# An encoder layer in one kernel: half of the first attention's probability blocks turned by VectorE and DRAM instead of TensorE, and twelve lower weight halves computed by GpSimd during the down-projection

## The chip, the cores and the metric

The kernel runs on one core of a Trainium2 chip. The metric is device time in microseconds (us), the median of the runs shown. The engines are called by the profile's names: PE is TensorE, DVE VectorE, ACT ScalarE, POOL GpSimd, SP SyncE (here it only issues DMAs).

## The reference

One layer of a bidirectional encoder, for two sequences of 512 tokens with 1024 features, in float32:

```python
x = x + 0.5 * swiglu(rms_norm(x, ffn1_norm), ffn1_w_gate, ffn1_w_up, ffn1_w_down)   # 1024 -> 2816 -> 1024
h = rms_norm(x, mix_norm)
proj = h @ w_in      # q, k, v of the attention; q, k, v, gates of the mLSTM; output gate; two merge gates
...
a = softmax(q k^T * scale) v      # 8 heads of 64, 2 key heads; RMS norm and rotary of q and k before
m = mlstm_bidirectional(...)      # 4 heads of 128
x = x + (sigmoid(g_att) * (a @ w_up_att) + sigmoid(g_mlstm) * (m @ w_up_mlstm)) @ w_out
x = x + 0.5 * swiglu(rms_norm(x, ffn2_norm), ffn2_w_gate, ffn2_w_up, ffn2_w_down)
```

followed by a last RMS norm.

## The kernel before, in words

**Arithmetic.** A float32 operand is split into an upper half `hi` (rounded to fp32r) and a lower half `lo = x - hi`; a product is three matmuls: hi by hi, hi by lo, lo by hi. ACT makes `hi` by a copy, DVE makes `lo` by a subtraction. For weights this is `fetch_w` (the load, L271) and `split_w` (L278 on ACT, L279 on DVE); for other tiles `split` (L715 on ACT, L716 on DVE).

**Stages.** Up-projection of the first feed-forward, its down-projection (437 to 648 us), the mixing block of sequence 0 (`mix(0)`), that of sequence 1 (`mix(1)`), output projection, second feed-forward. Weights of the mixing block are used by both sequences: `load_w` (L284) loads and splits a block for sequence 0 and stores both halves to DRAM (`wpark`, L303); sequence 1 loads them back (L293).

**Down-projection.** `ffn_down` (L548) runs 28 steps, four chunks of the inner dimension by seven products of a Strassen-like scheme. A step is a set of matmuls (L632), whose right operands `rt` come from DRAM four steps ahead (L566) and whose weights are split two steps ahead (`prep`). Sums are kept in SBUF tiles (`xs`, `e16`, `e5`). At step 7 it calls `mix_consts`, which loads and scales tables on POOL (L744 to L759). In its last seven steps `done1` receives finished rows of features; for both sequences POOL adds up their squares (L155), from which DVE (L225, L226) and PE (L232) make the row statistics that `mix` begins with.

**Attention.** In `mix(s)` the attention is written out by hand, and its PE instructions are pinned to the order of the program. Per head there are four query blocks of 128: `score` (L1096) does two matmuls (L1101), the row maximum on DVE (L1104), the exponential on ACT (L1106), the reciprocal on DVE (L1107), and the scaling of the probabilities by it, on ACT for odd query blocks (L1109), else on DVE (L1111). The product with V needs the probabilities turned, keys in the partitions, one key block at a time:

- `turn_keys` (L1114): four PE transposes (L1117) into PSUM, then the hi/lo split into SBUF. Sequence 0 does this for all four key blocks of each head.
- In sequence 1, only key blocks 2 and 3 go that way. For blocks 0 and 1, `turn_early` (L1129) turns 32 x 32 squares inside the partitions on DVE into part of the tile `box`; `send` (L1133) writes them to DRAM (`abuf`) with four DMAs of 128 KB from SP's queue, in an order of rows that completes the transposition; `fetch` (L1138) reads a key block back with a DMA of 256 KB from POOL's queue, and `parts` splits it from SBUF. A head's blocks 0 and 1 are used one head later in the loop.

`values` (L1148) multiplies with V: two matmuls per key block, one step behind the turn. Between these, `among(n)` issues n matmuls of the other projections (L825, "fill"); 8 per step, 24 per weight block. A step is one score, the fill, one turn and the product of the turn before; there are four per head. In sequence 0 the fill ends with head 6, block 1; the work of the mLSTM (L804, L1292) is placed between the rest by the scheduler.

The kernel is written with a tile framework: a scheduler places instructions by priority (`shifted` moves it), keeps the pinned ones in program order, and each engine then runs its own list in order. A DMA is issued by the engine whose queue holds it, so an instruction that waits in SP's list holds up all transfers behind it.

Of the kernel before, what the change touches and what calls it, by code (L numbers as in the profile page):

```python
# [16 lines left out]
P = 128  # L17
S = 512
# [8 lines left out]
def encoder(ctx, tc, I, outs):  # L27
# [91 lines left out]
    def f(ap):  # L119
        return ap.bitcast(F32)  # L120
# [160 lines left out]

    WEIGHTS = 60

    parked = {}  # L284

    def load_w(view, key, park=True):


        if key in parked:
            d, shape = parked[key]  # L290
            w2 = wpool.tile(shape, F32R, tag="w8", bufs=4, name=nm("w"))
            for i in range(2):
                nc.sync.dma_start(f(w2[:, i]), d[:, i])  # L293
            return w2[:, 0], w2[:, 1]
        raw = fetch_w(view)
        with shifted(-WEIGHTS):
            hi, lo = split_w(raw, V_)
        if not park:
            return hi, lo
        shape = [P, 2] + list(raw.shape[1:])  # L300
        parked[key] = d, _ = dpool.tile(shape, F32, name=nm("wpark")), shape
        for i, t in enumerate((hi, lo)):
            nc.sync.dma_start(d[:, i], f(t))  # L303
        return hi, lo
# [240 lines left out]
    DH = KD // 2  # L545
    n_steps = len(DOWN) * len(CHUNKS)

    def ffn_down(wd, rb, ring, tail, xres, done, at_step, hook, turned=None):  # L548
        n = n_steps
        rt = [A([P, 4, 2, S], F32R, "rt") for _ in range(3)]  # L550
        e16 = xs[2] = A([P, KD, S], F32, "e16")
        xs[0], xs[1] = A([P, KD, S], F32, "xs"), A([P, KD, S], F32, "xs")
        e5 = A([P, DH, S], F32, "e5")
        right = [[t[:, q] for q in range(3)] for t in rt] + [[t[:, 3] for t in rt]]
        w8 = [wpool.tile([P, 2, 2, S], F32R, tag="w8", bufs=4, name=nm("w")) for _ in range(4)]
        units = [t[:, i] for t in w8 for i in range(2)]
# [2 lines left out]
        free = [(0, t[:, 0:S], t[:, S:D]) for t in wr] + [(1, va, ha), (1, *v2)]  # L559
        s1s = ring.rows["s"]  # L560
        at = [0, 0]

        def load_right(i):
            if i < n:
# [131 lines left out]
        for i in range(n):  # L696
            if i == n - 1 and turned:
                products_turned(i)
            else:
                products(i, whole)  # L700
            prep(i + 2)
            load_right(i + 4)
            if i == 1:
                free.extend((1, *h4[k:k + 2]) for k in (0, 2))
                refill()
            if i == at_step:
                hook()

    def normed(xt, g, R, d):

# [137 lines left out]
    def mix(s, xh, xl, early=None, extra=None, after=None):  # L848
# [248 lines left out]
        def score(h, b):  # L1097
            hk = h // 4
            p = PS()
            for j in range(2):  # L1100
                pin(nc.tensor.matmul(p, qT[:, h, b * P:(b + 1) * P], kv[:, hk * 2 + j, :],  # L1101
                                     start=(j == 0), stop=(j == 1)))
            c = small(3, "asm")
            V_.tensor_reduce(c[:, 0:1], p, axis=AX.X, op=ALU.max, negate=True)  # L1104
            e = T2()
            nc.scalar.activation(e, p, AF.Exp, bias=c[:, 0:1], accum_out=c[:, 1:2])  # L1106
            V_.reciprocal(c[:, 2:3], c[:, 1:2])  # L1107
            if b % 2 and (s or h or b < 3):
                nc.scalar.activation(e, e, AF.Copy, scale=c[:, 2:3])  # L1109
            else:  # L1110
                V_.tensor_scalar(e, e, c[:, 2:3], None, op0=ALU.mult)  # L1111
            return e

        def turn_keys(Ps, kb):  # L1114
            p = PT()
            for b in range(4):
                pin(nc.tensor.transpose(p[:, b * P:(b + 1) * P], Ps[b][:, kb * P:(kb + 1) * P], ident))  # L1117
            return parts(p.rearrange("p (i a m) -> p a i m", i=4, a=4) if s else p)

        def parts(p):  # L1120
            ph, pl = T2(F32R), T2(F32R)
# [17 lines left out]
            return parts(p)  # L1139

        pos = {}
        KBS = (2, 3, 0, 1) if s else (0, 1, 2, 3)

        def values(h, kb, pp):
            if kb == KBS[0]:
                pos[h] = PO()
            for i, w in enumerate(pp):
                pin(nc.tensor.matmul(pos[h], Vst[:, kb, h // 4, :], w, start=(kb == KBS[0] and i == 0),  # L1148
                                     stop=(kb == KBS[3] and i == 1)))
            if kb != KBS[3]:  # L1150
                return
            po = pos.pop(h)
            order = ((lambda t: t.rearrange("p (a i m) -> p i a m", i=4, a=4)),
                     (lambda t: t.rearrange("p (i a m) -> p i a m", i=4, a=4))) if s else (lambda t: t,) * 2
            if h % 2 == 0:
                afs[0] = T2(F32, "f2")
            af = afs[0]
            o0 = (h % 2) * DA
            o1 = DA - o0
            t = T2(F32, "f2")  # L1160
            was, now = order
            nc.scalar.activation(now(t[o0:o0 + DA, :]), was(po[o1:o1 + DA, :]), AF.Copy)
            V_.tensor_tensor(now(af[o0:o0 + DA, :]), was(po[o0:o0 + DA, :]), now(t[o0:o0 + DA, :]), op=ALU.add)
            if h % 2:
                split(af, att[:, h // 2, 0, :], att[:, h // 2, 1, :])
# [20 lines left out]
        for b in range(4):  # L1186
            Ps.append(score(0, b))
            next(rope, None)
            among(FIRST[b])
        if s:  # L1190
            for i in range(2):
                turn_early(Ps[i], i)
        last = None
        for h in range(HA):
            nxt = []
            for b in range(4):
                if h in (0, 2, 4) and b == 2:
                    q_turn(h // 2 + 1, pin)
                if (h, b) == (0, 1):
                    gate_tops(*tops)  # L1200
                if (h, b) in ((0, 3), (2, 3)):
                    rope = q_rope(h // 2 + 2)
                if h < 4:
                    next(rope, None)
                if h + 1 < HA:
                    nxt.append(score(h + 1, b))
                if s and (h, b) != (HA - 1, 3) and b in (3, 0):
                    if b == 3:
                        for i in range(2):
                            turn_early(nxt[i], i)  # L1210
                    else:
                        for i in range(2, 4):
                            turn_early(Ps[i], i)
                if s and b == 1:
                    send(h)
                n0, n1_ = FILLER if b else SOON
                among(n0)
                pp = None
                if not s or b > 1:
                    pp = h, b, turn_keys(Ps, b)  # L1220
                elif h:
# [7 lines left out]
            Ps = nxt  # L1229
        for b in range(2 * s):  # L1230
            pp = HA - 1, b, fetch(HA - 1, b)
            among(sum(FILLER))
            values(*last)
            last = pp
# [515 lines left out]
        normed(xt, gm, R[1], d)  # L1750
        split(xt, nhl[1][0][:, d, :], nhl[1][1][:, d, :])

    ffn_down(I["ffn1_w_down"][0], rbuf[0], up.ring, tail, xbuf, done1, 7, mix_consts)


    box()
# [199 lines left out]
```

## Time and profile before

| | |
|---|---|
| median of 3 runs | 2035.45 us (2035.37 to 2037.29) |
| profiled execution: its own time | 2037.6 us |
| profiled execution: span of the trace | 2035.8 us |
| PE instructions | 9185 |
| first down-projection, from the first to the last product | 437.5 to 648 us |
| first attention, from the first turn to the last | 717.6 to 811.0 us |
| second attention, from the first turn on DVE | 1080.8 us on |

Times inside the program are counted from the start of the span. A row of a timeline gives start, duration, engine, line, operation, `written<-read` tiles, shapes and count. Matmuls are pipelined: the duration of one overlaps the next, so that their cost is the distance of their starts. In a row on idle time the engine waited for what stands behind the arrow. A row of the windows view gives, for a stretch of time, the busy time of each engine with its number of instructions, then the granted PE clock, the mean busy share of the DMA engines and GB/s. Rows of one line (`xN: min/median/max`) give durations in ns.

### The profile page before, as it was taken

How to read it: one execution, taken by the hardware profiler on the slowest of the kernel's cores; microseconds unless marked ns; L12 is line 12 of the kernel's file. 1: busy time of each engine (PE TensorE's matmuls, PEld its weight loads, DVE VectorE, ACT ScalarE, POOL GpSimd, SP SyncE). 2: the span in 40 equal slices, each digit the busy share in tenths (PEclk: the TensorE clock that was granted, in tenths of full speed). 3: DMA queues.
4: the chain of work that ended last, by engine and by line, in shares of the span. 5: the costliest groups of instructions: out<-in, count | busy, mean ns of one | idle time of the engine just before them, and what ended most of it. 6: DMA issues, size and time to landing. Idle time of an engine off the chain costs nothing.

```text
span 2035.8 us, 26777 instructions
## 1 busy us (share of the span) xinstructions
PE 2020.2 (99%) x9185; PEld 1665.7 (82%) x9185; DVE 1584.0 (78%) x2828; ACT 921.5 (45%) x1675; POOL 111.1 (5%) x148
## 2 busy tenths in 40 slices
PE   9999999999999999999999999999999999999998
PEld 7888888888888888888888877888888888888887
DVE  7988888886797798776566867467798988786797
ACT  7644444442234577653325654245444444442224
POOL 0000000001003000100120000011000000000001
PEclk9999999999999999999999999999999999999999
DMA  9656565799766954868656668877565655689753
GB/s 312 197 171 216 177 218 182 237 334 364 271 214 225 294 169 148 259 208 302 211 166 209 214 189 268 274 228 228 173 206 166 217 177 179 205 332 352 269 196 119
DMA packets 334696, 462.17 MB, mean 227 GB/s; under 512 B 21384, under 2 KB 207840, under 8 KB 333280
## 3 DMA queue, kind: packets, MB, share of 16 engines
q1 hardware_dynamic: 329920, 446.08, 65.8%
q0 software_dynamic: 4480, 14.11, 2.0%
q8 instruction: 72, 1.18, 0.2%
q14 instruction: 64, 0.52, 0.1%
q10 hardware_dynamic: 160, 0.27, 0.0%
HBM read 292.44 MB, written 167.94 MB: 226 GB/s over the span
## 4 chain that ended last, share of the span: by engine, by line
PE 91%; DVE 3%; DMA 3%; ACT 2%; issue 1%; SPq 0%; DVEq 0%; ACTq 0%
PE mm L839 13%; PE pso L374 12%; PE pst L374 12%; PE mm L374 10%; PE mm L632 9%; PE pss L374 6%; PE pst L632 4%; PE pss L632 4%; PE mm L825 4%; PE mm L804 3%; PE pso L632 3%; PE pso L1148 1%; PE pss L1101 1%; PE pst L839 1%; PE pss L839 1%; PE pso L1360 1%
## 5 line engine op out<-in xcount | busy, mean ns | idle before, releaser
L374 PE MATMUL pst<-xc,w 128*128 128x512 f32 x1056 | 253.8, 389 | 1.2 <-ACT t L409 1.2
L374 PEld LDWEIGHTS pst<-xc,w 128*128 128x128 f32 x1056 | 198.1, 188 | 42.7 <-ACT t L409 1.6
L374 PE MATMUL mm<-xc,w 128*128 128x512 f32 x972 | 229.6, 390 | 1.6 <-ACT f L382 1.6
L374 PEld LDWEIGHTS mm<-xc,w 128*128 128x128 f32 x972 | 182.0, 188 | 39.6 <-ACT f L382 2.1
L632 PE MATMUL mm<-rt,w 128*128 128x512 f32 x765 | 178.7, 389 | 0.0
L839 PE MATMUL mm<-xh,w 128*128 128x512 f32 x560 | 176.1, 391 | 1.4 <-DMA w<-wpark 1.4
L332 ACT ACTIVATE w<-t 128x512 fp32r<-128x512 f32 x176 | 106.5, 627 | 135.7 <-issue 63.1
L632 PEld LDWEIGHTS mm<-rt,w 128*128 128x128 f32 x765 | 143.5, 188 | 29.8
L333 DVE TENSOR_TENSOR w<-t,w 128x512 fp32r<-128x512 f32 x176 | 117.8, 688 | 40.9 <-ACT w L332 39.1
L374 PE MATMUL pso<-xc,f 128*128 128x512 f32 x528 | 127.0, 389 | 0.0
L374 PE MATMUL pss<-xc,w 128*128 128x512 f32 x528 | 126.8, 389 | 0.0
L374 PE MATMUL pso<-xc,w 128*128 128x512 f32 x528 | 126.8, 389 | 0.0
L839 PEld LDWEIGHTS mm<-xh,w 128*128 128x128 f32 x560 | 104.8, 188 | 23.7 <-DMA w<-wpark 1.8
L374 PEld LDWEIGHTS pso<-xc,f 128*128 128x128 f32 x528 | 99.0, 188 | 21.0 <-DVE t L413 0.4
L374 PEld LDWEIGHTS pso<-xc,w 128*128 128x128 f32 x528 | 99.1, 188 | 20.6
L374 PEld LDWEIGHTS pss<-xc,w 128*128 128x128 f32 x528 | 99.1, 188 | 20.6
L825 PE MATMUL mm<-xh,w 128*128 128x512 f32 x336 | 111.9, 398 | 0.0
L839 PE MATMUL mm<-xl,w 128*128 128x512 f32 x280 | 109.6, 391 | 0.0
L715 ACT ACTIVATE w<-wr 128x512 fp32r<-128x512 f32 x72 | 45.1, 632 | 138.4 <-PE pso L632 64.8
L278 ACT ACTIVATE w<-wr 128x1024 fp32r<-128x1024 f32 (+1 forms) x64 | 65.3, 1030 | 80.4 <-issue 24.5
L279 DVE TENSOR_TENSOR w<-wr,w 128x1024 fp32r<-128x1024 f32 (+1 forms) x64 | 79.8, 1247 | 26.6 <-ACT w L278 15.7
L715 ACT ACTIVATE w<-t 128x512 fp32r<-128x512 f32 x82 | 51.8, 632 | 107.4 <-PE pst L632 62.4
(457 smaller groups left out, 4080.4 us busy)
## 6 DMA issues: line engine op xcount, KB each, us to landing
rt<-rbuf SPq DMA_DIRECT2D x154, 512.0 KB, 5.4
wpark<-w SPq DMA_DIRECT2D x88, 512.0 KB, 3.6
w<-wpark SPq DMA_DIRECT2D x88, 512.0 KB, 5.3
wr<-in_ffn_w_gate_dram SPq DMA_DIRECT2D x62, 512.0 KB, 5.4
rbuf<-tab SPq DMA_DIRECT2D x102, 256.0 KB, 4.0
wr<-in_ffn_w_up_dram SPq DMA_DIRECT2D x44, 512.0 KB, 4.6
rbuf<-f SPq DMA_DIRECT2D x72, 256.0 KB, 4.2
wr<-in_w_in_dram SPq DMA_DIRECT2D x36, 512.0 KB, 5.7
```

Source lines behind the costliest of these rows:

```text
L278: pin(nc.scalar.activation(hi, raw, AF.Copy))
L279: pin(lo_eng.tensor_tensor(lo, raw, f(hi), op=ALU.subtract))
L332: pin(nc.scalar.activation(t[:, 0], src, AF.Copy))
L333: pin(V_.tensor_tensor(t[:, 1], src, f(t[:, 0]), op=ALU.subtract))
L374: nc.tensor.matmul(p, a[:, k, :], xt[:, b, k, :], start=(first and k == 0 and i == 0), stop=(k == HK_ - 1 and i == 2), skip_group_check=True)
L632: nc.tensor.matmul(p, u[:, a, d * P:(d + 1) * P], r[:, b, ts], start=(first and q == 0 and k == 0), stop=(q == len(us) - 1 and k == 2), sk ...
L715: nc.scalar.activation(hi, src, AF.Copy)
L804: mark(nc.tensor.matmul(p[b][:, :N], a[:, k, bs], w_[:, kl, :], start=(k == 0 and i == 0), stop=(k == KD - 1 and i == 2)), (kl, b, i) == ( ...
L825: pin(nc.tensor.matmul(p[0], a[:, k, :], b, start=(k == 0 and i == 0), stop=(k == n - 1 and i == 2)))
L839: mark(nc.tensor.matmul(p, a[:, k, :], b, start=(k == 0 and i == 0), stop=last), last)
L1101: pin(nc.tensor.matmul(p, qT[:, h, b * P:(b + 1) * P], kv[:, hk * 2 + j, :], start=(j == 0), stop=(j == 1)))
L1148: pin(nc.tensor.matmul(pos[h], Vst[:, kb, h // 4, :], w, start=(kb == KBS[0] and i == 0), stop=(kb == KBS[3] and i == 1)))
```

## The change

Three parts, all for sequence 0 (line numbers after the change are higher by 8 to 26):

1. **Turns.** In the first attention, heads 0 to 6 turn key blocks 0 and 1 as sequence 1 does: 28 turns on DVE, 28 sends, 14 fetches. Head 7 keeps PE transposes for all four blocks, blocks 0 and 1 behind the loop. The order of blocks in a head becomes 2, 3, 0, 1, and the copies out of PSUM permute the columns as in sequence 1.
2. **Scaling.** In sequence 0, heads 1 to 7 scale all four query blocks on ACT: 14 scalings move from DVE to ACT.
3. **Lower halves.** For twelve blocks of `w_in` (columns 896 and 1408, six gates of the attention, four output gates of the mLSTM) the lower half is computed in the down-projection of the first feed-forward, one block per step from step 3 on, by POOL: a load of 512 KB, a cast to fp32r (128x1024), a subtraction, a store of 512 KB to `wpark`. The space is the second half of the tile of `e5`, which is made twice as large. In `mix(0)`, `load_w` loads the block and splits off the upper half on ACT as before, but loads the lower half from `wpark` on SP instead of computing it on DVE, and stores only the upper half.

```diff
     def load_w(view, key, park=True):
...
         raw = fetch_w(view)
+        if key in lows:
+            d, shape = parked[key] = lows[key]
+            w2 = wpool.tile(shape, F32R, tag="w8", bufs=4, name=nm("w"))
+            nc.sync.dma_start(f(w2[:, 1]), d[:, 1])
+            with shifted(-WEIGHTS):
+                nc.scalar.activation(w2[:, 0], raw, AF.Copy)
+            nc.sync.dma_start(d[:, 0], f(w2[:, 0]))
+            return w2[:, 0], w2[:, 1]
         with shifted(-WEIGHTS):
             hi, lo = split_w(raw, V_)
...
-        e5 = A([P, DH, S], F32, "e5")
+        e5_ = A([P, KD, S], F32, "e5")
+        e5, spare = e5_[:, 0:DH], e5_[:, DH:KD].rearrange("p (i a) c -> p i (a c)", i=2)
...
+        def low_aside(view, key):
+            a, b = [spare[:, (len(aside) + i) % 2].rearrange("p (k c) -> p k c", c=view.shape[2]) for i in range(2)]
+            nc.gpsimd.dma_start(a, view)
+            G_.tensor_copy(b.bitcast(F32R), a)
+            G_.tensor_tensor(a.bitcast(F32R), a, b, op=ALU.subtract)
+            shape = [P, 2] + list(view.shape[1:])
+            lows[key] = d, _ = dpool.tile(shape, F32, name=nm("wpark")), shape
+            nc.gpsimd.dma_start(d[:, 1], a)
...
+            if i >= ASIDE and aside:
+                low_aside(*aside.pop(0))
+
+    ASIDE = 3
...
-            if b % 2 and (s or h or b < 3):
+            if b % 2 and (s or h or b < 3) or not s and h:
                 nc.scalar.activation(e, e, AF.Copy, scale=c[:, 2:3])
...
-        KBS = (2, 3, 0, 1) if s else (0, 1, 2, 3)
+        KBS = 2, 3, 0, 1
...
-        if s:
-            for i in range(2):
-                turn_early(Ps[i], i)
+        for i in range(2):
+            turn_early(Ps[i], i)
...
-                if s and (h, b) != (HA - 1, 3) and b in (3, 0):
+                if b in (3, 0) and h + b // 3 < (HA - 1 if not s else HA):
...
-                if s and b == 1:
+                if b == 1 and (h < HA - 1 or not (not s)):
                     send(h)
...
-                if not s or b > 1:
+                if b > 1:
                     pp = h, b, turn_keys(Ps, b)
                 elif h:
                     pp = h - 1, b, fetch(h - 1, b)
...
-        for b in range(2 * s):
-            pp = HA - 1, b, fetch(HA - 1, b)
+        for b in range(2):
+            pp = HA - 1, b, turn_keys(Ps, b) if not s else fetch(HA - 1, b)
...
-    ffn_down(I["ffn1_w_down"][0], rbuf[0], up.ring, tail, xbuf, done1, 7, mix_consts)
+    ffn_down(I["ffn1_w_down"][0], rbuf[0], up.ring, tail, xbuf, done1, 7, mix_consts,
+             aside=[(win_v[:, :, c:c + P], ("in", c)) for c in
+                    (896, 1408, *(2832 + d * P for d in range(2)), *(2320 + h * P for h in range(HM)),
+                     *(2832 + d * P for d in range(2, 6)))])
```

More of the change, by code (lines that the diff above doesn't have):

```diff
@@ L282, in encoder @@
     WEIGHTS = 60
-    parked = {}
+    parked, lows = {}, {}
     def load_w(view, key, park=True):
@@ L546, in encoder, with ffn_down @@
     n_steps = len(DOWN) * len(CHUNKS)
-    def ffn_down(wd, rb, ring, tail, xres, done, at_step, hook, turned=None):
+    def ffn_down(wd, rb, ring, tail, xres, done, at_step, hook, turned=None, aside=()):
         n = n_steps
@@ L561, in ffn_down @@
         at = [0, 0]
+        aside = list(aside)
+        def low_aside(view, key):
[6 more added lines that the diff above has]
+            nc.gpsimd.dma_start(d[:, 1], a)
         def load_right(i):
@@ L1117, in turn_keys @@
                 pin(nc.tensor.transpose(p[:, b * P:(b + 1) * P], Ps[b][:, kb * P:(kb + 1) * P], ident))
-            return parts(p.rearrange("p (i a m) -> p a i m", i=4, a=4) if s else p)
+            return parts(p.rearrange("p (i a m) -> p a i m", i=4, a=4))
         def parts(p):
@@ L1153, in values @@
             order = ((lambda t: t.rearrange("p (a i m) -> p i a m", i=4, a=4)),
-                     (lambda t: t.rearrange("p (i a m) -> p i a m", i=4, a=4))) if s else (lambda t: t,) * 2
+                     (lambda t: t.rearrange("p (i a m) -> p i a m", i=4, a=4)))
             if h % 2 == 0:
@@ L1228, in mix @@
                     extra[h - 2]()
-            Ps = nxt
-        for b in range(2 * s):
-            pp = HA - 1, b, fetch(HA - 1, b)
+            Ps = nxt or Ps
+        for b in range(2):
+            pp = HA - 1, b, turn_keys(Ps, b) if not s else fetch(HA - 1, b)
             among(sum(FILLER))
```

## The prediction

> **What bounds the kernel now.** First the page: span, engines, and the chain that ended last.
>
> ```profile
> span 2035.8 us, 26777 instructions
> PE 2020.2 (99%) x9185; PEld 1665.7 (82%) x9185; DVE 1584.0 (78%) x2828; ACT 921.5 (45%) x1675; POOL 111.1 (5%) x148
> PE 91%; DVE 3%; DMA 3%; ACT 2%; issue 1%; SPq 0%; DVEq 0%; ACTq 0%
> ```
>
> PE is idle for 15.6 us of 2035.8. A PE instruction taken away in a stretch without PE waits therefore shortens the span by its pitch, unless what replaces it makes PE wait. The view of waits, for PE between 640 us (end of the first down-projection) and 1180 us (end of the second attention), has one row:
>
> ```profile
> PE pso L1148 <- DVE t L716: 0.6, 1, 0.6
> ```
>
> The first attention (717 to 811 us) has no row at all; the one there is belongs to the second, which already works as the first shall work now. So the second attention is the nearest measurement of the change. Next, one step of the first attention on PE's timeline (columns: start, us, engine, line, tiles, count):
>
> ```profile
> 758.61 0.62 PE L1148 MATMUL pso<-t,kv 128*128 128x512 f32 x2
> 759.06 0.62 PE L1101 MATMUL pss<-kv,qT 128*128 128x512 f32 x2
> 759.53 0.62 PE L825 MATMUL mm<-xh,w 128*128 128x512 f32 x2
> 759.99 0.39 PE L825 MATMUL mm<-xl,w 128*128 128x512 f32 x1
> 760.22 0.62 PE L825 MATMUL mm<-xh,w 128*128 128x512 f32 x2
> 760.68 0.60 PE L1117 MATMUL pst<-ident,t 128*128 128x128 f32 x4
> 761.03 0.48 PE L825 MATMUL mm<-xl,w 128*128 128x512 f32 x1
> 761.34 0.63 PE L825 MATMUL mm<-xh,w 128*128 128x512 f32 x2
> 761.81 0.62 PE L1148 MATMUL pso<-t,kv 128*128 128x512 f32 x2
> ```
>
> A step is two products with V (L1148), two scores (L1101), eight fill matmuls (L825) and four transposes (L1117). Durations overlap, starts count: two matmuls follow each other 0.23 us apart, the transposes take 0.35 us (760.68 to 761.03), and the matmul behind them 0.31 instead of 0.23. The windows view of this step, and of a step of the second attention that has the same twelve matmuls without transposes (the counts include the one matmul that reaches in):
>
> ```profile
> core 0: us, PE busy (x) PEld busy (x) DVE busy (x) ACT busy (x) POOL busy (x), PEclk, DMA share, GB/s
> 758.61:761.81 3.20, 3.20 (x17) 2.64 (x16) 2.92 (x6) 2.44 (x6) 0.00 (x0) 1.00 0.00 0
> 1098.35:1101.08 2.73, 2.73 (x13) 2.25 (x12) 2.36 (x8) 2.43 (x7) 0.00 (x0) 1.00 0.02 9
> 720.00:800.00 80.00, 79.87 (x406) 65.42 (x405) 70.71 (x146) 58.63 (x116) 0.00 (x0) 1.00 0.46 158
> 1090.00:1170.00 80.00, 79.35 (x380) 65.18 (x380) 64.84 (x157) 54.41 (x114) 7.71 (x14) 1.00 0.69 207
> 440.00:600.00 160.00, 160.00 (x707) 132.49 (x706) 120.46 (x188) 46.33 (x76) 8.67 (x12) 1.00 0.80 289
> 600.00:626.00 26.00, 26.00 (x116) 21.52 (x116) 26.00 (x40) 10.42 (x17) 4.09 (x3) 1.00 0.66 219
> ```
>
> **The gain on PE.** Key blocks 0 and 1 of heads 0 to 6 lose their transposes: 14 sets of four. A set is worth 0.35 + 0.08 = 0.43 us by the timeline, 3.20 - 2.73 = 0.47 by the windows; I take 0.45, so 14 x 0.45 = 6.3 us (6.0 to 6.6). PE's order of instructions, head 2, steps of block 1, before (tiles: pst transposes, mm fill, pso products with V):
>
> ```order
> L825 MATMUL mm_6222<-xh_4898,w_6113 128x512
> L825 MATMUL mm_6222<-xl_4899,w_6113 128x512
> L825 MATMUL mm_6222<-xh_4898,w_6113 128x512 x2
> L825 MATMUL mm_6222<-xl_4899,w_6113 128x512
> L1117 MATMUL pst_6285<-ident,t_515_6101 128x128
> L1117 MATMUL pst_6285<-ident,t_527_6145 128x128
> L1117 MATMUL pst_6285<-ident,t_534_6175 128x128
> L1117 MATMUL pst_6285<-ident,t_540_6204 128x128
> L825 MATMUL mm_6222<-xh_4898,w_6113 128x512 x2
> L825 MATMUL mm_6222<-xl_4899,w_6113 128x512
> L1148 MATMUL pso_6297<-t_552_6259,kv_5279 128x512
> L1148 MATMUL pso_6297<-t_553_6260,kv_5279 128x512
> ```
>
> and the same step after (L849 is the fill, L1172 the product with V):
>
> ```order
> L849 MATMUL mm_6255<-xh_4958,w_6151 128x512
> L849 MATMUL mm_6255<-xl_4959,w_6151 128x512
> L849 MATMUL mm_6255<-xh_4958,w_6151 128x512 x2
> L849 MATMUL mm_6255<-xl_4959,w_6151 128x512
> L849 MATMUL mm_6255<-xh_4958,w_6151 128x512 x2
> L849 MATMUL mm_6255<-xl_4959,w_6151 128x512
> L1172 MATMUL pso_6269<-t_550_6292,kv_5339 128x512
> L1172 MATMUL pso_6269<-t_551_6293,kv_5339 128x512
> ```
>
> The transposes are gone and nothing has come in their place; the product now takes the previous head's block 0, which came back from DRAM. The last head keeps its four sets; two of them now stand behind the loop, among other work.
>
> **What DVE and ACT get for it.** The rows of the turn, the scaling on DVE and on ACT, and the lower half of a weight block:
>
> ```profile
> L1129 DVE STREAM_TRANSPOSE box<-t x32: 393/428/446, 1080.8 to 1172.8; 128x256 f32<-128x256 f32 x32
> L1111 DVE TENSOR_SCALAR t<-t,asm x33: 477/486/491, 710.0 to 1168.7; 128x512 f32<-128x512 f32 x33
> L1109 ACT ACTIVATE t<-t,asm x31: 709/721/725, 711.2 to 1171.7; 128x512 f32<-128x512 f32 x31
> L279 DVE TENSOR_TENSOR w<-wr,w x64: 702/1225/2306, 639.8 to 1369.8; 128x1024 fp32r<-128x1024 f32 x60, 128x544 fp32r<-128x544 f32 x4
> ```
>
> Per head DVE gains four turns (4 x 0.43 = 1.7 us), and loses two scalings (1.0) and about 1.6 lower halves (one per three steps of 3.2 us; 1.6 x 1.2 = 2.0). ACT gains two scalings (1.4). Between 720 and 800 us DVE was busy 70.71 of 80, ACT 58.63. A head was 13.2 us there (six heads in 717.6 to 797.0) and becomes 13.2 - 0.9 = 12.3: DVE 11.7 - 1.3 = 10.4 of 12.3 (85%, from 88%), ACT 9.7 + 1.4 = 11.1 of 12.3 (90%, from 73%). So the lower halves, taken away in advance, make room on DVE for the turns, and ACT becomes the fuller one. Before, PE ran without waits beside DVE at 88%; I expect small waits beside ACT at 90%, not a new bound.
>
> **The way through DRAM.** Landing times, of the sends (L1133) and of the fetches (L1138), min/median/max; and from the page, parked weight blocks:
>
> ```profile
> DMA to landing us min/median/max: 2.0/2.5/3.2
> ...
> DMA to landing us min/median/max: 2.8/4.1/6.0
> ...
> w<-wpark SPq DMA_DIRECT2D x88, 512.0 KB, 5.3
> ```
>
> From a head's sends at block 1 to the product that uses them lie four steps, 4 x 2.7 to 3.2 = 11 to 12 us. Needed: four issues of some 0.5 us (2), 2.5 to land, an issue (0.5), 4.1 to land, the split on ACT and DVE (1.4): 10.5. The reserve of 1 us is thin, and is used up when a send waits in SP's queue. SP's order after, at heads 2 and 3 (L1157 sends, L299 loads a lower half, L302 stores the upper half, L271 loads a block):
>
> ```order
> L1157 DMA abuf_261<-box_5338 32x8x128 x4
> L299 DMA w_6354<-wpark_4375 128x1024
> L302 DMA wpark_4375<-w_6354 128x1024
> L271 DMA wr_6687<-in_w_in_dram 128x8x128
> L271 DMA wr_7091<-in_w_in_dram 128x2x512
> L1157 DMA abuf_262<-box_5338 32x8x128 x4
> ```
>
> Before, there stood in this place:
>
> ```order
> L303 DMA wpark_6435<-w_6432 128x1024 x2
> L303 DMA wpark_6547<-w_6544 128x1024 x2
> L271 DMA wr_7085<-in_w_in_dram 128x2x512
> ```
>
> Each store waits for ACT's upper half, and behind it the next head's sends; ACT at 90% makes that later. Lower halves arrive 5.3 us behind their issue, where a block of fill is 24 matmuls or three steps, over 8 us; they move as many bytes as the store that they replace. Over the seven heads 28 sends of 128 KB and 14 fetches of 256 KB come on top: 7.3 MB in 86 us, 85 GB/s on 158. The DMA share of 0.46 becomes 0.71; the second attention ran at 0.69 with one wait, in the row
>
> ```profile
> 1126.30 0.50 PE L1148 MATMUL pso<-t,kv 128*128 128x512 f32 x1 [0.65 <-DVE t L716]
> ```
>
> That is a price from this trace for such an attention: 0.65 us. Bounds: nothing (reserve holds) and, for the case that every one of 14 fetched blocks comes half a microsecond late, 7 us. I take 1.1, near the measured row, with something for ACT: **net 6.3 - 1.1 = 5.2 us.**
>
> **The lower halves on POOL.** In the down-projection POOL does twelve rounds of load, cast, subtraction and store. Rows: PE's first product there; POOL's idle time before; one of its loads there, with its time to land; POOL's adds of the row statistics behind it, first and last; and the step that waits for them.
>
> ```profile
> L632 PEld LDWEIGHTS mm<-rt,w x765: 187/188/192, 437.5 to 2009.9; 128*128 128x128 f32 x192
> 467.88 0.60 POOL L744 DMA_DIRECT2D tab<-in_c_tri_dram  x1 [134.76 <-DMA wr<-in_ffn_w_down_dram]
> f<-in_c_rope_dram POOLq DMA_DIRECT2D x1, 256.0 KB, 6.9
> 605.31 1.30 POOL L155 TENSOR_TENSOR R<-R,f 128x512 f32<-128x512 f32 x1 [116.70 <-ACT f L154]
> 635.17 1.29 POOL L155 TENSOR_TENSOR R<-R,f 128x512 f32<-128x512 f32 x1 [0.88 <-ACT f L154]
> 637.24 0.69 DVE L226 TENSOR_REDUCE row<-f 128x16 f32<-128x512 f32 x1
> 643.13 0.29 PE L232 MATMUL pst<-row,fold 128*128 128x16 f32 x2
> ```
>
> In POOL's order four rounds stand ahead of the tables (L744) and the last seven ahead of those adds. The trace has no round. An issue 0.6, landing 6.9, the cast between 1.3 and 2.6 (an add of half its width takes 1.3), the subtraction 2.6, a store's issue 0.6: 12.0 to 13.3, and up to 16 if landing and arithmetic are a fifth slower in company. Twelve of them and 9 us for the tables, from 438 us: the end lies at 591 to 607, or 639. The adds need 9.1 us (7 x 1.3) behind it if all are late, then 1.4 for DVE's two steps; PE asks at 643.1. So an end up to 632.6 us costs nothing: I put this part at **nothing**, covered by POOL's idle time. Without the cover it costs a microsecond per microsecond.
>
> The rounds move 12.6 MB, 79 GB/s over 160 us, on 289 GB/s at a DMA share of 0.80: about 1.0. The fullest part of the down-projection was that already, and PE had no wait in it:
>
> ```profile
> 440.00:497.00 57.00, 57.00 (x253) 47.18 (x252) 41.82 (x64) 22.28 (x38) 8.67 (x12) 1.00 0.98 367
> ```
>
> So the traffic should stretch POOL's own landings, which pushes the end toward the later values, rather than starve PE. What else touches another engine is this pair of rows:
>
> ```profile
> 630.63 1.30 POOL L155 TENSOR_TENSOR R<-R,f 128x512 f32<-128x512 f32 x1 [0.85 <-ACT f L154]
> 631.27 1.21 DVE L716 TENSOR_TENSOR w<-t,w 128x512 fp32r<-128x512 f32 x1
> ```
>
> DVE's subtraction ended (632.48) 0.55 behind POOL's add (631.93): it took 1.21 us where its other calls take 0.69. The Trainium skill, page "SBUF — State Buffer", section "Who interferes with whom", says why: a DVE instruction with two SBUF inputs contends with a GpSimd instruction that reads SBUF, and the one that comes second is blocked entirely. The trace agrees. By rows: twelve rounds keep POOL reading for 12 x 3.9 to 5.2 = 47 to 62 us; if DVE lost half of that, it would be busy some 147 of the 160 us from 440 to 600, where it was 120, and still have idle time. From 600 to 626 DVE has no idle time at all; rounds that fall there delay it by up to 5 us each.
>
> **The sum.** The profiled run took 2037.6 us (span 2035.8), 2.15 over the median of 2035.45. Taking 5.2 from both: span 2030.6, and for the median 2035.45 - 5.2 = **2030.3**.
>
> **The rivals.**
> 1. *The way through DRAM is late.* Stores in front of the sends wait for ACT, fetches miss their step, PE waits some 0.2 to 0.4 us at each of 14 products: 3 to 6 us, net gain 0 to 3.3, time 2032 to 2035.5. For it: a reserve of 1 us, ACT at 90%. Against it: one wait in the second attention. Chance 0.25.
> 2. *Slower: POOL ends late.* At 16 us a round the end is 639 and takes 6.4 us from PE, so that the gain is gone; from 638 on the kernel is slower than before. With 17.5 us a round it is 657: 24 us lost, time 2055. The half-way case, 645, gives 12.4 lost, 2042.6. The lock of the last rows speaks for it, since DVE and POOL work all the time there; POOL's 117 us without work speak against it. Chance 0.10.
> 3. *The transposes were hidden*, and the change does nothing on PE: then 2035. The step of 3.20 against 2.73 excludes nearly all of it; chance 0.02.
>
> The forecast has 0.63. A measurement of this kernel tells 0.2%, 4.1 us, from no change: faster means under 2031.4, a net gain over 4.1, hence waits under 2.2 us. Chances: faster 0.63, same 0.27, slower 0.10. The range reaches from the full 6.6 us (2028.8) to rival 1's upper part: 2028.7 to 2035.0.
>
> **What would show it.** Right: PE x9129 (56 fewer) and busy 6.3 us less; steps of block 0 and 1 of 2.7 us; no PE wait between 640 and 717; the last round on POOL over before 632; ACT near 90% from 720 to 800. Wrong: rows of waits on PE at the product with V (L1172) for ACT or DVE splits of fetched tiles, which is rival 1; a PE wait at the row statistics (L232) or any in 440 to 640, which is rival 2.

## The result and the profile after

The change makes the kernel slower: 2042.02 us (median of 19 runs, 2036.07 to 2046.92) against 2035.17 us for before (19 runs, 2033.37 to 2037.29), a ratio of 1.0032, 95% interval 1.0025 to 1.0039. Forecast were 2030.3 us, range 2028.7 to 2035.0. The profiled execution of after took 2042.34 us. The page of after:

```profile
span 2040.6 us, 26831 instructions
PE 2017.4 (99%) x9129; PEld 1659.7 (81%) x9129; DVE 1587.8 (78%) x2830; ACT 930.2 (46%) x1689; POOL 181.3 (9%) x210
```

The 56 transposes are gone (x9129) and PE is busy 2.8 us less, but it is idle for 23.2 us where it was 15.6. The view of waits for PE has rows in two stretches where before had none but one, from 440 to 640 us and from 640 to 1180 us (engine, tile, line, releaser: us in total, times, longest):

```profile
PE mm L652 <- issue: 2.1, 1, 2.1
PE pss L652 <- ACT w L739: 1.3, 1, 1.3
PE mm L652 <- DVE w L740: 0.9, 1, 0.9
...
PE pso L1172 <- DVE t L740: 1.6, 4, 0.7
PE pso L828 <- DVE f L1187: 1.5, 1, 1.5
PE pss L1315 <- DVE t L1331: 1.3, 1, 1.3
PE pso L1172 <- DVE f L1187: 1.2, 1, 1.2
```

Where the time went is read best from the start of one and the same PE instruction in both traces:

| place | before | after | after - before |
|---|---|---|---|
| first product of the down-projection | 437.76 | 437.36 | -0.40 |
| first matmul of the mixing block | 647.46 | 653.18 | +5.72 |
| first attention, block 1 of head 6 (the score of head 7) | 798.17 | 799.99 | +1.82 |
| projections behind the last head | 842.92 | 847.00 | +4.08 |
| a later projection of the mixing block | 871.62 | 876.88 | +5.26 |

So 6.1 us are lost in the down-projection, 3.9 won back in the loop over the heads, and 3.4 lost again behind it. The new order of blocks also moves four products with V (0.9 us) from the loop to behind it, so the loop without this would have won less, and the stretch behind it lost less. The two traces differ by 4.8 us at the end (2040.6 against 2035.8), 2 less than the medians, since the profiled run of before was 2.4 us above its median.

**Down-projection.** Three of POOL's twelve subtractions, the first, one in the middle and the last, and the last store, on its timeline:

```profile
444.42 2.73 POOL L578 TENSOR_TENSOR e<-e 128x1024 fp32r<-128x1024 f32 x1
...
540.66 2.38 POOL L578 TENSOR_TENSOR e<-e 128x1024 fp32r<-128x1024 f32 x1
...
603.94 2.72 POOL L578 TENSOR_TENSOR e<-e 128x1024 fp32r<-128x1024 f32 x1
606.96 0.57 POOL L581 DMA_DIRECT2D wpark<-e  x1 [0.30 <-POOL e L578]
```

The last round is over at 607.5, the late end of the estimate of 591 to 607. POOL is not late. DVE beside these subtractions, and then PE at its three longest waits of the stretch:

```profile
444.98 2.71 DVE L446 TENSOR_TENSOR t<-t,tab 128x512 fp32r<-128x512 f32 x1
...
541.41 2.18 DVE L614 TENSOR_TENSOR t<-wr,t 128x512 f32<-128x512 f32 x1 [5.68 <-DMA t<-in_ffn_w_down_dram]
...
546.52 0.68 DVE L685 SCALAR_TENSOR_TENSOR e<-mm,e 128x512 f32<-128x512 f32 x1
...
605.52 4.70 DVE L674 TENSOR_TENSOR xs<-xs,e 128x512 f32<-128x512 f32 x6
```

```profile
448.35 4.61 PE L652 MATMUL mm<-rt,w 128*128 128x512 f32 x19 [0.86 <-DVE w L740]
...
547.30 6.37 PE L652 MATMUL mm<-rt,w 128*128 128x512 f32 x27 [2.10 <-issue]
...
619.94 2.32 PE L652 MATMUL pss<-rt,w 128*128 128x512 f32 x9 [1.25 <-ACT w L739]
```

Two things make DVE late. One is the lock of the prediction: a DVE instruction that meets POOL's subtraction takes longer. At 444.98 it takes 2.71 us (0.69 in before), nearly until the subtraction ends at 447.15, and the split that PE waits for at 448.35 stands behind it in DVE's order. The other is a late load, and at 541.41 both meet: DVE stands 5.68 us for a weight load, its instruction then takes 2.18 us, since POOL's subtraction holds it until 543.04, and what stands behind it is late too, up to the instruction at 546.52, which empties the bank of PSUM (`mm`) that PE needs at 547.30. Behind 600 us DVE has no idle time in which to catch up: beside the last cast and subtraction it falls back by 1.9 us against before (the six sums from 605.52 take 4.70 us, in before 3.69), and PE waits at 619.94. Against before, PE loses 1.1 us at the first of the three waits, 2.3 at the second, 1.4 at the third, and the rest of the 6.1 in smaller steps.

The loads land later than before, in fuller queues. Transfers issued from 440 to 600 us (KB each, median us from issue to landing), before:

```profile
rt<-rbuf SPq DMA_DIRECT2D x59, 512.0 KB, 5.1
t<-in_ffn_w_down_dram SPq DMA_DIRECT2D x18, 256.0 KB, 4.9
```

and after, with the windows row of the same stretch (PE, PEld, DVE, ACT, POOL busy, PEclk, DMA share, GB/s):

```profile
rt<-rbuf SPq DMA_DIRECT2D x56, 512.0 KB, 9.5
t<-in_ffn_w_down_dram SPq DMA_DIRECT2D x18, 256.0 KB, 7.2
440.00:600.00 160.00, 156.78 (x689) 128.56 (x688) 125.71 (x178) 44.42 (x73) 66.35 (x56) 1.00 0.98 357
```

DVE is idle for 34 us of these 160, and PE waits all the same: a mean share of busy time does not say whether the one instruction that PE needs is in time.

**Attention.** One step with transposes and one without, from product to product, head 2 of after:

```profile
741.44 0.62 PE L1172 MATMUL pso<-t,kv 128*128 128x512 f32 x2
...
744.63 0.62 PE L1172 MATMUL pso<-t,kv 128*128 128x512 f32 x2
...
747.38 0.62 PE L1172 MATMUL pso<-t,kv 128*128 128x512 f32 x2
```

3.19 and 2.75 us: a set of transposes is worth 0.44 here. The loop has lost 13 sets by 800 us, 5.7 to 6.1 us, and gained 3.9. PE's waits there add up to 2.1; the two longest are the first two rows here, and the third row is from behind the loop (PE; below it DVE at the second row):

```profile
758.29 0.74 PE L1172 MATMUL pso<-t,kv 128*128 128x512 f32 x2 [1.15 <-DVE f L1187]
...
787.35 0.50 PE L1172 MATMUL pso<-t,kv 128*128 128x512 f32 x1 [0.46 <-DVE t L740]
...
821.43 0.73 PE L828 MATMUL pso<-w,xh 128*128 128x512 f32 x2 [1.47 <-DVE f L1187]
```

```profile
785.96 0.76 DVE L1153 STREAM_TRANSPOSE box<-t 128x256 f32<-128x256 f32 x2
786.64 0.65 DVE L740 TENSOR_TENSOR t<-pst,t 128x512 fp32r<-128x512 f32 x1
```

The second is a block turned by PE, whose split stands behind two of the new turns in DVE's order. The first waits for the copy that empties the one bank for the products. Only two products in the loop wait for the split of a fetched block, 0.23 us each. The late block costs more behind the loop: the sends of head 6, the fetch, and the splits on ACT and DVE:

```profile
799.74 1.84 SPq L1157 DMA_DIRECT2D abuf<-box  x4
...
804.94 1.07 POOL L1162 DMA_DIRECT2D f<-abuf  x2 [10.40 <-DVE asm L1131]
...
811.29 0.63 ACT L739 ACTIVATE t<-f 128x512 fp32r<-128x512 f32 x1 [1.56 <-DMA f<-abuf]
811.95 0.69 DVE L740 TENSOR_TENSOR t<-f,t 128x512 fp32r<-128x512 f32 x1 [2.03 <-ACT t L739]
```

From 799.74 to 812.64 are 12.9 us, where 10.5 were estimated and 11 to 12 were there. PE doesn't stand still at that product; it takes matmuls of the mLSTM first. It then waits 1.47 us at 821.43 (the row above), where the next projection needs the bank that head 7's last product leaves, and 1.28 at 864.18.

### The profile page after: what moved, and what is told of

It reads as the page before. It is cut to its first block, busy times and chain, and to the rows that moved or that the text cites. A ratio compares the mean times of both kernels' runs of the same rounds, so it can differ in the third digit from the quotient of the medians.

```text
span 2040.6 us, 26831 instructions
## 1 busy us (share of the span) xinstructions
PE 2017.4 (99%) x9129; PEld 1659.7 (81%) x9129; DVE 1587.8 (78%) x2830; ACT 930.2 (46%) x1689; POOL 181.3 (9%) x210
## 4 chain that ended last, share of the span: by engine, by line
PE 89%; DVE 4%; ACT 3%; DMA 2%; issue 1%; SPq 0%; DVEq 0%; ACTq 0%
PE mm L863 14%; PE pso L382 11%; PE pst L382 11%; PE mm L382 10%; PE mm L652 7%; PE pss L382 6%; PE pss L652 4%; PE mm L849 4%; PE pst L652 4%; PE mm L828 4%; PE pso L652 2%; PE pso L1172 1%; PE pss L1125 1%; PE pst L863 1%; PE pss L863 1%; PE pso L1383 1%
## 5 line engine op out<-in xcount | busy, mean ns | idle before, releaser
L652 PE MATMUL pss<-rt,w 128*128 128x512 f32 x396 | 94.0, 390 | 1.3 <-ACT w L739 1.3
L652 PE MATMUL pst<-rt,w 128*128 128x512 f32 x396 | 93.6, 389 | 0.0
```

Of the source, the lines that this page charges most:

```text
L652: nc.tensor.matmul(p, u[:, a, d * P:(d + 1) * P], r[:, b, ts], start=(first and q == 0 and k == 0), stop=(q == len(us) - 1 and k == 2), sk ...
```

## The experiments

Medians, before on the same chip, and the ratio with its 95% interval:

| label | what it is | us | before | ratio |
|---|---|---|---|---|
| turns_only | parts 1 and 2 | 2040.49 | 2035.21 | 1.0022 [1.0013, 1.0030] |
| rounds_only | part 3 | 2040.54 | 2035.21 | 1.0028 [1.0017, 1.0040] |
| rounds_traffic | before, rounds without arithmetic | 2044.64 | 2035.21 | 1.0041 [1.0028, 1.0055] |
| rounds_math | before, rounds without traffic | 2052.31 | 2035.21 | 1.0090 [1.0076, 1.0104] |
| rounds_six_early | before, six rounds from 438 us | 2037.11 | 2035.15 | 1.0010 [1.0001, 1.0019] |
| rounds_six_late | before, six rounds from 506 us | 2035.27 | 2035.62 | 1.0003 [0.9994, 1.0013] |
| turns_free | parts 1 and 2 without turns, sends, fetches | 2030.86 | 2035.62 | 0.9979 [0.9970, 0.9989] |
| turns_cut | turns and fetches made, not waited for | 2035.58 | 2035.15 | 1.0004 [0.9995, 1.0012] |
| turns_two_on_pe | turns_only, last two heads on PE | 2038.49 | 2035.62 | 1.0013 [1.0003, 1.0022] |
| all_two_on_pe | the change, last two heads on PE | 2040.18 | 2035.62 | 1.0021 [1.0012, 1.0031] |
| six_late_two_on_pe | the same, and six late rounds | 2034.70 | 2035.15 | 1.0003 [0.9994, 1.0011] |
| six_late_two_scaled | that, scaling as before | 2038.85 | 2035.15 | 1.0017 [1.0008, 1.0025] |
| six_late_two_pool_sends | that, sends from POOL | 2042.94 | 2036.23 | 1.0032 [1.0021, 1.0044] |
| six_late_two_lag | that, products two steps behind | 2035.20 | 2035.80 | 0.9998 [0.9989, 1.0007] |

### The two halves of the change

`turns_only` leaves out part 3 (`load_w` and `ffn_down` as before); `rounds_only` leaves out parts 1 and 2.

> Parts 1 and 2 alone: the turns, the way through DRAM and the scaling on ACT in the first attention; no rounds on POOL, the twelve lower halves on DVE in the mixing block as before. Theory A (the rounds on POOL cost the down-projection 6.1 us; the attention gains only what its own waits leave, 0.5 us): no PE wait between 437 and 648, the end of the down-projection at 648, and 2034 to 2036. If DVE, with some 97% of the first attention, becomes the bound, up to 2039. Theory B (the rounds cost nothing in themselves, the loss lies in the attention): about 2041 as with the whole change.

> Part 3 alone: twelve rounds on POOL in the down-projection and lower halves loaded in the mixing block; the first attention as before, with all transposes on PE. Theory A: 6 us of waits in the down-projection and nothing gained, 2041. Theory B: 2035.

Each half alone costs 5.3 us. In the trace of `rounds_only` PE is 2.0 us ahead of before at the first product of the down-projection and 5.0 behind at its end, so it loses 7.1 us there. Three of its waits from 440 to 640 us (at 446.67, 544.81 and 619.26) are where after has its three; the longest, at 605.40, stands behind sums of DVE that beside the last round take 5.53 us for four:

```profile
PE mm L652 <- DVE e L685: 1.4, 1, 1.4
PE pss L652 <- ACT w L739: 1.3, 1, 1.3
PE mm L652 <- issue: 1.0, 2, 0.8
PE mm L652 <- DVE w L740: 0.8, 1, 0.8
PE mm L652 <- DMA rt<-rbuf: 0.5, 1, 0.5
```

`turns_only` has no wait there. Against before it stands at -4.1 us at 747, -2.2 at 797, +0.8 at 843 and +1.3 at 872: it wins in the loop and loses it behind the loop. Its profiled run was the fastest of its runs (2036.40), so 4 us of its median are not in this trace.

### What in the rounds costs

The arithmetic goes, the transfers stay; or the transfers shrink to 32 columns of one block, and the arithmetic stays. In both the rounds' results are used by nothing.

```diff
 rounds_traffic
-            G_.tensor_copy(b.bitcast(F32R), a)
-            G_.tensor_tensor(a.bitcast(F32R), a, b, op=ALU.subtract)
+            G_.memset(a, 0.0)
+            for _ in range(3):
+                G_.memset(b, 0.0)
 rounds_math
-            nc.gpsimd.dma_start(a, view)
+            nc.gpsimd.dma_start(a[:, 0:1, 0:32], view[:, 0:1, 0:32])
...
-            nc.gpsimd.dma_start(d[:, 1], a)
+            nc.gpsimd.dma_start(d[:, 1, 0:1, 0:32], a[:, 0:1, 0:32])
```

> The kernel before, with rounds in the down-projection whose results nobody uses: each loads 512 KB and stores 512 KB, and in place of the cast and the subtraction POOL only writes (four memsets of 128x1024), so that it reads nothing from SBUF. If the waits come from the traffic alone (weights and right operands of the down-projection land late): 2041. If they come from POOL's reads, which hold DVE's subtractions up: 2035.5. I expect the two to share it, 2037.

> The kernel before, with rounds whose results nobody uses: cast and subtraction of 128x1024 on POOL as in the change, but a load and a store of only 128 x 128 bytes each, so that hardly any bytes move. If POOL's reads are the cause: 2041. If the traffic is: 2035.5. I expect 2038.

Traffic alone is enough for a loss, of 9.4 us in the median and of 6.9 in the down-projection by the trace: a `w_down` load then lands 10.1 us behind its issue, and PE has waits of 2.4 us for DVE and 1.8 us for `rt`. But it loses at other places (481, 501 and 549 us). At 447, 605 and 619 us, where `rounds_only` loses 1.1 and 3.3, it loses nothing: there the loss needs POOL's arithmetic. So both cost, late loads and the lock. The same stretch, `rounds_traffic` and then `rounds_only`:

```profile
437.00:600.00 163.00, 157.41 (x690) 128.90 (x689) 113.75 (x182) 44.81 (x74) 69.58 (x84) 1.00 0.98 361
```

```profile
437.00:600.00 163.00, 160.68 (x705) 131.69 (x704) 131.62 (x183) 46.45 (x77) 66.97 (x58) 1.00 0.97 356
```

As many DVE instructions (182, 183) are busy 18 us longer beside casts and subtractions than beside memsets. The rule of the Trainium skill, "SBUF — State Buffer", section "Who interferes with whom", draws the line there too: GpSimd instructions that read SBUF block two-input DVE instructions, those that only write don't. `rounds_math` doesn't measure the change's arithmetic: a memset ahead of its rounds let them begin at 395 us, in the up-projection, and PE had lost 10.2 us by its first product of the down-projection. It does show the lock without the traffic, in another 8.5 us in the down-projection: a DVE instruction at 461.52 us takes 2.73 us beside POOL's subtraction, and PE waits 2.35 at 464.90. The granted clock, at 0.50 for 3.4 us twice in this run, is a part of these losses.

The other way to ask is to halve the rounds and to place them. Both kernels have the first six rounds of the list; a copy on POOL from the residual's tile makes the late one wait for DVE's sum of step 8:

```diff
+            if len(aside) == 5:
+                G_.tensor_copy(a[:, 0, 0:1], xs[0][:, 0, 0:1])
...
-    ASIDE = 3
+    ASIDE = 8
```

> The kernel before with six rounds, the same as those begun late, but begun at 438 us as in the change. If it matters where a round runs (full DMA queues and DVE's sums from 438 to 500): 2037 to 2038. If six rounds cost nothing wherever they run, and only the later ones of the twelve do: 2035.3.

> The kernel before with six rounds instead of twelve, begun after the tables on POOL and after step 8, at about 503 us, so that they miss the fullest stretch of the DMA queues and end by 590, before DVE is busy all the time. The attention is as before. If a round costs the same wherever it runs: 2035.2 + 5.3 / 2 = 2037.9. If it is the collision with full queues and with the full DVE that costs: 2035.5.

From 438 us on, six rounds cost 2 us; from 506 to 586 us they are free. The stretch before 497 us already had a DMA share of 0.98 without them, but what the early ones lose by the trace, 1.3 us, comes from the lock: their loads land as late as in after (7.2 us for `w_down`), without a wait of PE for them. PE's only wait in the down-projection stands behind a DVE instruction that the first subtraction holds for 2.71 us:

```profile
448.95 2.34 PE L652 MATMUL mm<-rt,w 128*128 128x512 f32 x9 [0.91 <-DVE w L740]
```

`rounds_six_late`, landing and the windows row:

```profile
rt<-rbuf SPq DMA_DIRECT2D x59, 512.0 KB, 6.6
t<-in_ffn_w_down_dram SPq DMA_DIRECT2D x18, 256.0 KB, 6.1
437.00:600.00 163.00, 163.00 (x721) 134.97 (x720) 128.88 (x191) 46.96 (x78) 39.87 (x37) 1.00 0.91 330
```

PE is busy for all 163 us, beside the same lock: a DVE instruction takes 2.88 us at 543 us, but DVE has idle time behind it, and the loads land in 6.1 us, not 7.2.

### What in the turns costs

`turns_free` makes no turns, sends and fetches in sequence 0, and its products of blocks 0 and 1 use block 3's halves; `turns_cut` makes them all, and its products still use block 3's halves, so that nothing waits for the way through DRAM.

```diff
                 if b > 1:
                     pp = h, b, turn_keys(Ps, b)
+                    kept = pp[2]
                 elif h:
                     pp = h - 1, b, fetch(h - 1, b)
+                    if not s:
+                        pp = h - 1, b, kept
```

(`turns_cut`; in `turns_free` the `fetch` isn't made either.)

> Parts 1 and 2 without rounds, and with nothing in the transposes' place: in heads 0 to 6 key blocks 0 and 1 are neither turned, sent, fetched nor split; the product with V takes block 3's halves once more, so that the output is wrong and only the time is read. Theory C (the gain on PE is there, and the turns' replacement eats it, by waits in the loop and behind it): 2035.2 - 6.3 = 2029. Theory D (the loss comes with the new order itself, block order 2, 3, 0, 1 and the last head behind the loop, whatever feeds the products): 2032 to 2038.

> Parts 1 and 2 without rounds, all turns, sends, fetches and splits in place, but PE's products of blocks 0 and 1 in heads 0 to 6 take block 3's halves once more instead of the fetched ones (the output is wrong; only the time is read). PE then never waits for a fetched tile itself. Theory E (the products wait because the way through DRAM is a step too long): the loop's loss goes, and the time is that of the kernel without replacement, 2031 to 2033. Theory F (DVE and ACT, each in its own order, are held up by the turns, the splits and the fetches in their queues, and everything behind comes late): it stays near 2039 to 2040.5.

Without the turns most of the gain is there: -4.83 us against before at 843, 2030.86 us in the median, 4.8 less than before. The expectation for it was 2029, since the forecast of 2030.3 holds 1.1 us of waits that this kernel shouldn't have; a part of what is missing is a wait for the single bank of the products, 1.20 us at 752.95, which the change has too (1.15 at 758.29) and which so doesn't come from the turns. `turns_cut` divides the loss. In the loop it is at -2.6 at 797, like `turns_only` (-2.2): the loop's loss comes from DVE's and ACT's added work and its order, and from that bank. Behind the loop it keeps -2.1 at 843, where `turns_only` has +0.8: most of that loss is the way through DRAM. The windows of the loop, of `turns_free` and of `turns_cut`:

```profile
720.00:800.00 80.00, 78.40 (x376) 63.66 (x375) 60.98 (x128) 65.05 (x124) 0.00 (x0) 1.00 0.50 170
```

```profile
720.00:800.00 80.00, 76.35 (x363) 60.91 (x362) 72.52 (x161) 67.91 (x131) 6.52 (x13) 1.00 0.75 236
```

If the late way is the end's loss, another head on PE should mend it:

```diff
-                if b in (3, 0) and h + b // 3 < (HA - 1 if not s else HA):
+                if b in (3, 0) and h + b // 3 < (HA - 2 if not s else HA):
...
-                    pp = h - 1, b, fetch(h - 1, b)
+                    pp = h - 1, b, fetch(h - 1, b) if s or h - 1 < HA - 2 else turn_keys(before, b)
```

> Parts 1 and 2 without rounds, with the last two heads on PE instead of one: 12 sets fewer than before instead of 14, and no fetch is pending when the fill ends. If the tail's loss (some 3 us between 797 and 843 us) comes from waiting for the last fetches without fill: 2040.5 + 0.9 - 3 = 2038.4. If it comes from the two turns behind the loop, it stays: 2041.4.

> The whole change, with the last two heads on PE instead of one. As before: 2042.0 + 0.9 - 3 = 2040 if the last fetches are what the tail waits for, 2043 if the turns behind the loop are.

Both are some 2 us better than with one head on PE, and slower than before. In `turns_two_on_pe` the stretch behind the loop costs 2.1 us (-3.45 to -1.33) instead of 3.0, although two more sets of transposes (0.9 us) stand there.

### The change, mended

`six_late_two_on_pe` is the whole change with six late rounds and the last two heads on PE. `six_late_two_scaled` gives DVE back its half of the scalings (part 2 undone).

> The whole change with the two mends that the runs so far point to: six rounds from 503 us on (three gates of the attention, three output gates of the mLSTM) and the last two heads on PE. Down-projection without loss; the attention as with the last two heads on PE without rounds, 2038.5, less what six lower halves relieve DVE, some half of 3.8: 2036.5. If the relief of those six is all that the loop lacks: 2034.

> The same with the scaling as before, every second query block on DVE instead of all on ACT. If ACT's fill is what makes the loop wait: 2034.5, faster than with the scaling on ACT. If DVE's is: 2039, slower.

The mended kernel takes 2034.70 us, some 7 less than the change and no different from before. Its waits from 640 to 1180 us:

```profile
PE pso L1174 <- DVE t L742: 1.5, 5, 0.6
PE pso L1174 <- DVE f L1189: 1.5, 2, 1.2
PE pss L1317 <- DVE t L1333: 0.4, 1, 0.4
```

The longest of the first row, 0.6 us, is in the second attention, where before has it too.

Part 2 is right: undone, it costs 4 us, so DVE, not ACT, is the engine with too much in the loop.

The last two kernels go for these waits: the sends from POOL's queue, past SP's; or the products two steps behind the turns instead of one.

```diff
 six_late_two_pool_sends
-                nc.sync.dma_start(abuf[h % 2][:, :, a, :].rearrange("n r x -> r n x"),
+                (nc.sync if s else nc.gpsimd).dma_start(abuf[h % 2][:, :, a, :].rearrange("n r x -> r n x"),
 six_late_two_lag
-        last = None
+        last, lag = [], 1 if s else 2
...
-                if last:
-                    values(*last)
-                last = pp
+                if len(last) == lag or last and not pp:
+                    values(*last.pop(0))
+                if pp:
+                    last.append(pp)
```

> Six rounds from 503 us on, the last two heads on PE, and the sends of the first attention issued from POOL's queue instead of SP's, where they stand behind stores that wait for ACT and loads that wait for a free slot. If SP's queue is what makes the fetched tiles late: 2033 or less, faster than before. If it is the length of the way itself (four issues, two landings, a split): 2034.7 as with the sends on SP, or more, since POOL's queue then waits for DVE ahead of the fetches.

> Six rounds from 503 us on, the last two heads on PE, sends on SP as in the change; and in the first attention every product with V comes two steps behind its turn or fetch instead of one. If the way through DRAM is simply longer than the four steps it is given: the products find their tiles, and the time is that of the cut kernel or less, 2032 to 2033, faster than before. If DVE and ACT come late whatever the products wait for: 2034.7 as without.

POOL's queue is worse by 7 us: in the first attention a send lands 2.4 to 8.0 us behind its issue (median 5.0), and 2.2 to 4.7 (2.9) from SP in the change, and PE waits for splits up to 1.95 us. With the lag no product of the first attention waits for a split any more (the 0.6 is the second attention's), and the wait for the single product bank takes their place; the sum is about the same:

```profile
PE pso L1174 <- DVE f L1189: 2.7, 3, 1.6
PE pso L1174 <- DVE t L742: 0.6, 1, 0.6
```

None of the fourteen is faster than before but `turns_free`, which leaves out the turns.

## Why the prediction was wrong, step by step

- **The gain on PE** was right: 0.45 us a set forecast, 0.44 measured above, and `turns_free` keeps 4.8 us of the forecast 6.3. That its time is near 2030.3 is in part luck.
- **The lower halves on POOL** is the step that failed: "I put this part at nothing, covered by POOL's idle time." It cost 6.1 us in after's trace and 5.3 us alone. The end of the rounds was estimated right, but POOL's time was not what counted: what POOL did to the loads and to DVE was. "The traffic should stretch POOL's own landings [...] rather than starve PE" drew on a stretch with a DMA share of 0.98 and no wait; the share says that the queues are full, not how long a load then stands in them, and that rose from 4.9 to 7.2 us for a weight block; once DVE stood 5.68 us for one. The lock was seen, but priced by DVE's mean ("and still have idle time"), where what counts is one held instruction in an ordered queue: at 444.98 its 0.69 us became 2.71, and PE waited 0.86 us behind it. The working also says that rounds from 600 to 626 us delay DVE by up to 5 us each, and has them end at 591 to 607, but gives that no price; the last round delayed DVE by 1.9 us, and PE lost 1.4.
- **The waits in the attention** were put at 1.1 us. The trace has 2.1 in the loop and 2.75 behind it, and of the 6.2 us of the fourteen sets (0.44 each) some 0.5 are left at 877 us, the down-projection aside, 0.9 less than these waits explain. ACT became the fuller one, as forecast, 82% busy from 720 to 800 us (90% forecast) against DVE's 79% (85%), but "small waits beside ACT" failed:

```profile
720.00:800.00 80.00, 77.93 (x368) 62.43 (x367) 63.42 (x151) 65.76 (x129) 6.47 (x12) 1.00 0.79 244
```

  PE waited for DVE. The second attention was the wrong measure for the end: by the code, the last head's PE transposes and splits stand there in sequence 0 and not in sequence 1.
- **The lower halves taken from DVE** were right to count: the loop gained 1.7 us in `turns_only` and 3.9 in the change, by the traces.
- **Rival 1** (late way through DRAM) came true behind the loop, 12.9 us for 10.5 (the fetch took 5.6 of it, for 4.1), and in the loop at two of the 14 products, with 0.23 us each. **Rival 2** had the sign of a wait from 440 to 640 us, and its half-way case of 2042.6 is near the measured time by luck, since its mechanism is not the one: POOL was done at 607.5, in time for the row statistics, and PE waited in the products before and beside it. **Rival 3** is out by `turns_free`.

What stays open: of `turns_only`'s 5.3 us the trace of its fastest run shows 1.3 by 872 us, and at the end of the span it is 1.2 us ahead of before's. Seven of its other ten runs had a mean granted clock of 0.997 or 0.998 against 0.999, but the three with 0.999 took 2040.80 to 2042.52 us, so the clock isn't the whole reason; the cause of some 4 us of its median is not shown. The 3.8 us by which the two halves together (10.6) exceed the whole (6.85) have the same uncertainty.

## What to carry to other kernels

An idle engine is no cover for work that brings traffic: ask how long the other loads of that stretch take to land under it, what its reads hold up on other engines, and which instruction in an ordered queue stands behind the latest of these. Place such work where loads have time to catch up and the engine that is held has idle time; half of it, moved by 68 us, was free here. Where PE is never idle, work taken off it only counts once the engines that take it over meet every due time of a step, and the last item of a pipeline, with nothing behind it to fill the wait, is better left on the short way.

## What the runs showed of the hardware

Outside the change, in the mixing block of sequence 1, PE waits for parked weights at two places close together, in before as well (1.41 us). In some runs the granted clock falls there. `turns_two_on_pe`, timeline of PE and windows row (PEclk third from the end):

```profile
1223.86 0.50 PE L839 MATMUL mm<-xh,w 128*128 128x512 f32 x1 [0.31 <-DMA w<-wpark]
...
1225.98 0.74 PE L839 MATMUL mm<-xh,w 128*128 128x512 f32 x2 [1.38 <-DMA w<-wpark]
...
1225.00:1230.00 5.00, 4.02 (x11) 3.18 (x12) 0.00 (x0) 0.00 (x0) 0.00 (x0) 0.67 1.04 364
```

and before, the same window:

```profile
1225.00:1230.00 5.00, 3.82 (x17) 3.17 (x18) 0.00 (x0) 0.00 (x0) 0.00 (x0) 1.00 1.01 359
```

Eleven matmuls instead of 17 in 5 us: behind waits of 1.7 us together the granted clock is 0.50 for 3.4 us, and from 1226.2 to 1229.5 PE falls back by 1.6 us against before. The Trainium skill, "TensorE: Matmul & The Clock Gate", section "HAM oscillation — how this bites in real kernels", sets the limit at idle gaps of some 3.4 us; here the clock fell behind two gaps of 0.31 and 1.38 us, and by the measurement the rule is too wide. The length of a gap alone doesn't decide: a single wait of 2.16 us was followed by such a fall in `rounds_traffic`, and waits of 1.87 us in after and 2.04 in `six_late_two_lag` were not. What decides stays open.
